# Thirteen down tiles of a PEER layer split in two parts instead of six

## The chip, the cores and the metric

The kernel runs on one core of a Trainium2 chip. The time is the device time of one execution in microseconds; before the change the median of three runs is 1321.99 us (1321.54 to 1322.99).

In what follows TensorE (PE) multiplies matrices, VectorE (DVE), ScalarE (ACT) and GpSimd (POOL) work elementwise, and SyncE (SP) issues most of the loads.

## The reference, cut to what matters

Two blocks run one behind the other on a sequence of 256 tokens with 1024 features, all in float32. The change lies in the last layer of the second block, a PEER layer: for each token eight heads pick 16 of 16384 one-neuron experts each.

```
qry = (ht @ w_query).reshape(T, 8, 2, 128)
sub_scores = einsum('thpc,hpkc->thpk', qry, sub_keys)
top_s, top_i = top_k(sub_scores, 16)
cand_s = top_s[:, :, 0, :, None] + top_s[:, :, 1, None, :]
best_s, best_c = top_k(cand_s.reshape(T, 8, 256), 16)
gate = softmax(best_s)
a = einsum('pd,ped->pe', xb, expert_down[ib])
act = gelu(a) * gb
y = einsum('pe,ped->pd', act, expert_up[ib])
```

## The kernel before

The kernel doesn't gather experts. It multiplies all 16384 rows of `expert_down` with all 256 tokens, in 128 tiles of 128 experts (a down tile), takes the Gelu, multiplies by a dense matrix G that holds each token's gates and is zero elsewhere, and multiplies with all rows of `expert_up`.

A float32 product comes in two forms. In the split form an operand is cut into an upper part `hi` (ScalarE, a copy to the type fp32r, line 218) and a lower part `lo` (GpSimd, source minus `hi`, line 220), and three matmuls per block of 128 features add hi by hi, hi by lo and lo by hi (`mm3`, lines 285 to 287). The layer's input stands in SBUF so already, as `xh` and `xl` (in the trace xTh and xTl). In the full-precision form one float32 matmul per block is issued (line 1561), straight from the loaded tile `dst`; its input is `xf`, the sum of `xh` and `xl`, made in four pieces by GpSimd (`xf_part`, line 1695).

The order around the change is the order in which the program is written; each engine runs its instructions in it.

- Query heads 0 to 7 (`q_mm`, `q_score`): TensorE makes scores, VectorE finds the best 16 (`top16`: MAX8, FIND_INDEX8, MATCH_REPLACE8), and GpSimd adds the candidate sums of an earlier head (`best_sums`, lines 1510 and 1513, four small instructions a head). The sums of the last head, 7, are VectorE's. Meanwhile GpSimd makes lower parts of query weights and of down tiles 0 and 1, and three of the four pieces of `xf`.
- Down tiles 0 to 11 (`down_step`, `NPRE` = 12). Step n first issues the split of tile n + 2, a half at a time, if n + 2 is below `SPLIT`, then the matmuls of tile n and its Gelu (line 1569). With `SPLIT` = 6, tiles 0 to 5 are split and tiles 6 to 25 full-precision. Upper and lower parts lie in four buffers each.
- Beside these steps, VectorE turns the chosen candidates into keys (`best_keys`): TENSOR_SCALARs of 128x128 (lines 1523 to 1528 and 1535) and predicated copies that walk down a binary tree (lines 1531 and 1540). Behind step 8 ScalarE takes the Exp of the gates (line 1487), and VectorE divides by their sum (lines 1489 to 1491).
- Behind tile 11, TensorE transposes keys and gates (`to_slots`, lines 1496 and 1497); ScalarE and VectorE (line 1504) copy them out.
- Tile 12, and then the one-hot rows: VectorE builds them in float16 (lines 1620 and 1627), TensorE multiplies them to G (line 1640), with down tiles 13 to 25 in between, a half tile at a time.
- From tile 26 on (`LEAD` = 26) a loop over all 128 tiles takes a split down tile and an up tile in each turn.

Of the kernel before, what the change touches and what calls it, by code (L numbers as in the profile page):

```python
# [32 lines left out]
    _off += _w  # L33
NCST = _off
LEAD = 26
SPLIT = 6


VEC = {}
# [45 lines left out]
def block_kernel(ctx: ExitStack, tc, a, dump=None, stop=None):  # L85
# [814 lines left out]
    def q_load(g):  # L900
        st = strm.tile([P, 8, 256], F32, tag="st", name=nm("st"))
        sp.dma_start(st, wq[:, g * 256:(g + 1) * 256].rearrange("(p j) n -> p j n", j=8))
        qprep[g] = st
# [12 lines left out]
    def q_split(g):  # L916
        q_hi(g)
        q_lo(g, 0, pool if g > 1 else vec)
        q_lo(g, 1)
# [331 lines left out]
    for s in range(28):  # L1251
        i, g = divmod(s, 2)
# [70 lines left out]
    for s in range(28, 36):  # L1323
        i, g = divmod(s, 2)
# [103 lines left out]
    def q_mm(g):  # L1428
        pr = qprep.pop(g)
        o = (MM if g else PSM)([P, 2, T])  # L1430
        for kk in (range(0, 4), range(4, 8)):
            for part, x in ((0, xh), (1, xh), (0, xl)):
                for k in kk:
                    for m in range(2):
                        pe.matmul(o[:, m, :], pr[k // 4][part][:, k % 4, m * P:(m + 1) * P], x[:, k, :],  # L1435
                                  start=k == 0 and m == 0 and part == 0 and x is xh,
                                  stop=k == KD - 1 and x is xl, skip_group_check=True)
        act.activation(qTs[g % 2], o, AF.Copy)
# [15 lines left out]
    def q_score(g):  # L1454
        sps = PSM([P, 2, 2, P])
        for tt in range(2):
            for i in range(2):
                pe.matmul(sps[:, tt, i, :], qTs[g % 2][:, i, tt * P:(tt + 1) * P], skT[:, g * 2 + i, :],
                          start=True, stop=True)
        sc = scr[g % 3]  # L1460
        act.activation(sc, sps, AF.Copy)
        top16([(tv[tt][:, g * 2 + i, :], ti[tt][:, g * 2 + i, :], sc[:, tt, i, :])
               for tt in range(2) for i in range(2)])
# [42 lines left out]
    def best_sums(h, eng):  # L1506

        for b in best:
            v0, v1 = tv[b.tt][:, 2 * h, :], tv[b.tt][:, 2 * h + 1, :]
            eng.tensor_tensor(b.cd[:, h, 0:64].rearrange("p (x y) -> p x y", x=4),  # L1510
                              v0[:, 0:4, None].to_broadcast([P, 4, 16]),
                              v1[:, None, :].to_broadcast([P, 4, 16]), op=ALU.add)
            eng.tensor_tensor(b.cd[:, h, 64:112].rearrange("p (x y) -> p x y", x=12),
                              v0[:, 4:16, None].to_broadcast([P, 12, 4]),
                              v1[:, None, 0:4].to_broadcast([P, 12, 4]), op=ALU.add)

    def best_top(h):
        top16([(b.bs[:, h, :], b.bc[:, h, :], b.cd[:, h, :]) for b in best])

    def best_keys(best):  # L1520

        for b in best:
            vec.tensor_scalar(b.g64, b.bc, 64, None, op0=ALU.is_ge)
            vec.tensor_scalar(b.rk[0], b.bc, 4, None, op0=ALU.logical_shift_right)
            vec.tensor_scalar(b.r2[0], b.bc, 2, None, op0=ALU.logical_shift_right)
            vec.tensor_scalar(b.rk[1], b.bc, 15, None, op0=ALU.bitwise_and)
            vec.tensor_scalar(b.r2[1], b.bc, 3, None, op0=ALU.bitwise_and)
            vec.tensor_scalar(b.r2[0], b.r2[0], 12, None, op0=ALU.subtract)
        for b in best:
            for side in range(2):  # L1530
                vec.copy_predicated(b.rk[side], b.g64, b.r2[side])
        for side in range(2):
            for b in best:
                for bi, w in enumerate((8, 4, 2, 1)):
                    vec.tensor_scalar(b.bit[bi], b.rk[side], w, None, op0=ALU.bitwise_and)
            for bi, w in enumerate((8, 4, 2, 1)):
                for b in best:
                    tree = b.tree[side]
                    data = b.tfh[:, :, side, None, 8:16].to_broadcast([P, 8, 16, 8]) if w == 8 else tree[:, :, :, w:2 * w]
                    vec.copy_predicated(tree[:, :, :, 0:w], b.bit[bi][:, :, :, None].to_broadcast([P, 8, 16, w]), data)  # L1540


    def down_load(i):
        st = strm.tile([P, 2, KD, P], F32, tag="st", name=nm("dst"))
        sp.dma_start(st.rearrange("p a k e -> p (a k e)"), down_w[i // 2])
        dload[i], dload[i + 1] = st[:, 0], st[:, 1]

    def down_split(i, half=None):
        if half != 1:
            dprep[i] = (dload.pop(i), *HL([P, KD, P]))  # L1550
        dT, hi, lo = dprep[i]
        s = slice(0, 8) if half is None else slice(half * 4, half * 4 + 4)
        split(hi[:, s, :], lo[:, s, :], dT[:, s, :], lo="pool")
# [139 lines left out]
    def xf_part(i):  # L1693
        s = slice(2 * i, 2 * i + 2)
        pool.tensor_tensor(xf[:, s], xh[:, s].bitcast(F32), xl[:, s].bitcast(F32), op=ALU.add)
# [4 lines left out]
    for g in range(8):  # L1700
        if g + 2 < 8:
            q_load(g + 2)
        else:
            down_load(2 * g - 12)
        if g + 1 < 8:
            q_split(g + 1)
        else:
            down_split(0)
        q_mm(g)
        if g > 1:  # L1710
            best_sums(g - 2, pool)
        if g == 7:
            xf_part(0)
            xf_part(1)
        if g:
            q_score(g - 1)
        if g > 1:
            best_top(g - 2)
    down_split(1)
    best_sums(6, pool)  # L1720
    xf_part(2)
    q_score(7)
    best_top(6)
    best_sums(7, vec)
# [3 lines left out]
    NPRE, N_COPY, N_GATE = 12, 3, 8  # L1728

    def down_step(n):  # L1730

        if n % 2 == 0 and n + 4 < LEAD:
            down_load(n + 4)
        yield
        if n + 2 < SPLIT:
            down_split(n + 2, 0)
        down_mm(n, 0)
        yield
        if n + 2 < SPLIT:
            down_split(n + 2, 1)  # L1740
        down_mm(n, 1)
        dload.pop(n, None)
        down_act(n)
        if n == LEAD - 3:
            down_load(LEAD)
        if n == LEAD - 2:
            up_load(0)
        yield

    for n in range(NPRE):  # L1750
        for part, _ in enumerate(down_step(n)):
            if part and 0 < n - N_COPY <= 2:
                best[part - 1].leaves(n - N_COPY - 1)
        if n == 1:
            xf_part(3)
        if n == N_COPY:
            for b in best:
                b.copies()
        if n == N_COPY + 2:
            best_keys(best)  # L1760
        if n == N_GATE:
            for b in best:
                b.gates()
# [84 lines left out]
    for tt in range(2):  # L1848
        for hf in range(2):
            n = 2 if tt and hf else 1  # L1850
# [30 lines left out]
```

## Time and profile before

| | us |
|---|---|
| median of three runs | 1321.99 |
| the profiled execution | 1321.84 |
| its span, first to last instruction | 1320.1 |
| TensorE busy in it | 1290.4 |
| VectorE busy | 828.7 |
| ScalarE busy | 675.8 |
| GpSimd busy | 381.7 |

Times in the trace count from the start of the span. The stages around the change are: query heads to about 537 us, down tiles 0 to 11 from 537 to 578, one-hot rows with tiles 12 to 25 from 578 to 657, then the loop over the 128 tiles. A row of the timeline has the start, the time taken, the engine, the line, the operation with output and inputs, and the count of instructions that were merged into it; in brackets stands the idle time ahead of it and the engine that ended it. A duration includes the time in which an instruction that has been started waits for a resource. Instructions on one engine overlap a little, so the pace is read from their starts.

### The profile page before, as it was taken

The numbers are of one execution on the slowest core, as the hardware profiler recorded it, in microseconds if no ns is written. First come the engines' busy times: TensorE is split into PE (matmuls) and PEld (weight loads), VectorE is DVE, ScalarE is ACT, GpSimd is POOL, SyncE is SP. The second block draws the span as 40 slices with busy tenths as digits, with TensorE's granted clock in tenths as the row PEclk, the third lists the DMA queues.
The fourth block names the chain that finished last, engine by engine and source line by source line (L and its number), as shares of the span: only waits on it lengthen the run. The fifth ranks groups of instructions, "written<-read, shape, count | busy, mean of one in ns | idle before, by whom it ended". The sixth has DMA issues, their size and how long they took to land.

```text
span 1320.1 us, 20727 instructions
## 1 busy us (share of the span) xinstructions
PE 1290.4 (98%) x8176; PEld 1141.3 (86%) x8176; DVE 828.7 (63%) x1522; ACT 675.8 (51%) x1146; POOL 381.7 (29%) x219
## 2 busy tenths in 40 slices
PE   7999999999999999999999999999999999999998
PEld 6877899977777879988889999999999999999886
DVE  6868788766866768989974754333333333333676
ACT  7755554544665454536654444544444444444442
POOL 0101111011212128700154444443444444444100
PEclk9999999999999999999999999999999999999999
DMA  9526679865564365346555665665555755455653
GB/s 302 200 81 238 222 257 299 304 245 192 170 208 162 125 187 166 129 141 201 193 210 214 229 228 194 244 255 192 192 191 187 276 210 179 178 185 191 214 184 112
DMA packets 103538, 266.73 MB, mean 202 GB/s; under 512 B 6873, under 2 KB 50571, under 8 KB 94993
## 3 DMA queue, kind: packets, MB, share of 16 engines
q1 hardware_dynamic: 93376, 255.32, 55.2%
q10 hardware_dynamic: 10064, 10.09, 2.3%
q8 instruction: 64, 1.05, 0.3%
q14 instruction: 34, 0.27, 0.1%
HBM read 254.90 MB, written 10.49 MB: 201 GB/s over the span
## 4 chain that ended last, share of the span: by engine, by line
PE 82%; DVE 9%; ACT 3%; issue 2%; DMA 2%; POOL 1%; ACTq 0%; SPq 0%; DVEq 0%; POOLq 0%
PE mm L287 12%; PE mm L286 12%; PE mm L285 12%; PE mm L299 9%; PE psm L285 7%; PE psm L287 7%; PE psm L286 7%; PE psm L1561 5%; PE mm L1640 2%; PE mm L758 2%; DVE lo L222 2%; DMA aw<-in_ada_w_dram 1%; PE mm L1435 1%; ACT hi L218 1%; DVE s L1448 1%
## 5 line engine op out<-in xcount | busy, mean ns | idle before, releaser
L220 POOL TENSOR_TENSOR lo<-dst,hi 128x1024 fp32r<-128x1024 f32 (+1 forms) x113 | 269.6, 2388 | 419.8 <-ACT hi L218 419.8
L1585 DVE TENSOR_TENSOR lo<-ust,hi 128x1024 fp32r<-128x1024 f32 x128 | 165.0, 1289 | 341.2 <-ACT hi L1580 341.2
L285 PE MATMUL psm<-xTh,hi 128*128 128x256 f32 x864 | 244.6, 283 | 0.0
L287 PE MATMUL psm<-xTh,lo 128*128 128x256 f32 x864 | 242.7, 281 | 1.7 <-POOL lo L220 1.5
L286 PE MATMUL psm<-xTl,hi 128*128 128x256 f32 x864 | 244.1, 282 | 0.0
L1580 ACT ACTIVATE hi<-ust 128x1024 fp32r<-128x1024 f32 x128 | 135.7, 1060 | 207.9 <-DMA ust<-in_peer_up_dram 108.5
L285 PE MATMUL mm<-hi,og 128*128 128x512 f32 x512 | 202.2, 395 | 1.2 <-ACT og L1596 1.2
L286 PE MATMUL mm<-lo,og 128*128 128x512 f32 x512 | 202.9, 396 | 0.0
L287 PE MATMUL mm<-hi,og 128*128 128x512 f32 x512 | 202.5, 396 | 0.3 <-DVE og L1601 0.3
L222 DVE TENSOR_TENSOR lo<-st,hi 128x1024 fp32r<-128x1024 f32 x127 | 157.8, 1264 | 61.6 <-ACT hi L218 61.4
L218 ACT ACTIVATE hi<-st 128x1024 fp32r<-128x1024 f32 x127 | 132.1, 1055 | 101.6 <-PE mm L299 47.0
L287 PEld LDWEIGHTS psm<-xTh,lo 128*128 128x128 f32 x864 | 164.2, 190 | 2.5 <-POOL lo L220 2.5
L285 PEld LDWEIGHTS psm<-xTh,hi 128*128 128x128 f32 x864 | 161.8, 187 | 4.8
L286 PEld LDWEIGHTS psm<-xTl,hi 128*128 128x128 f32 x864 | 162.2, 188 | 4.2
L1569 ACT ACTIVATE ga<-psm 128x256 f32<-128x256 f32 x128 | 49.0, 383 | 150.9 <-PE psm L287 123.8
L287 PEld LDWEIGHTS mm<-hi,og 128*128 128x128 f32 x512 | 96.2, 188 | 23.7 <-DVE og L1601 0.9
L218 ACT ACTIVATE hi<-dst 128x1024 fp32r<-128x1024 f32 (+1 forms) x113 | 114.1, 1014 | 0.9 <-ACT gst L1647 0.9
L285 PEld LDWEIGHTS mm<-hi,og 128*128 128x128 f32 x512 | 96.2, 188 | 20.0 <-ACT og L1596 1.4
L286 PEld LDWEIGHTS mm<-lo,og 128*128 128x128 f32 x512 | 96.2, 188 | 18.8
L1589 DVE TENSOR_TENSOR oj<-ga,G 128x256 f32<-128x256 f32 x128 | 92.4, 722 | 1.3 <-ACT G L1643 1.3
L1561 PE MATMUL psm<-xf,dst 128*128 128x256 f32 x320 | 75.0, 383 | 0.0
L1561 PEld LDWEIGHTS psm<-xf,dst 128*128 128x128 f32 x320 | 58.5, 190 | 6.8
(448 smaller groups left out, 2157.1 us busy)
## 6 DMA issues: line engine op xcount, KB each, us to landing
dst<-in_downT_dram SPq DMA_DIRECT2D x64, 1024.0 KB, 6.8
ust<-in_peer_up_dram SPq DMA_DIRECT2D x64, 1024.0 KB, 4.9
st<-in_w_in_dram SPq DMA_DIRECT2D x25, 1024.0 KB, 5.9
st<-in_w_gate_up_dram SPq DMA_DIRECT2D x22, 1024.0 KB, 7.7
aw<-in_ada_w_dram SPq DMA_DIRECT2D x40, 512.0 KB, 5.6
st<-in_w_down_dram SPq DMA_DIRECT2D x11, 1024.0 KB, 4.8
st<-in_w_out_dram SPq DMA_DIRECT2D x8, 1024.0 KB, 5.0
st<-in_peer_w_query_dram SPq DMA_DIRECT2D x8, 1024.0 KB, 5.8
```

The source lines that it names most:

```text
L218: act.activation(dst_hi, src, AF.Copy)
L220: pool.tensor_tensor(dst_lo, src, dst_hi.bitcast(F32), op=ALU.subtract)
L222: vec.tensor_sub(dst_lo, src, dst_hi.bitcast(F32))
L285: pe.matmul(out, lh, rh, start=start, stop=False, **kw)
L286: pe.matmul(out, lh, rl, start=False, stop=False, **kw)
L287: pe.matmul(out, ll, rh, start=False, stop=stop, **kw)
L299: pe.matmul(o[:, m, :], wk(k)[part][:, m * P:(m + 1) * P], x[:, k, :], start=k == 0 and m == 0 and part == 0 and x is xh, stop=k == KD - 1 ...
L1561: pe.matmul(gas[i], dload[i][:, k, :], xf[:, k, :], start=k == 0, stop=k == KD - 1)
L1569: act.activation(ga, gas[i], AF.Gelu)
L1580: act.activation(hi, st, AF.Copy)
L1585: vec.tensor_sub(lo, st, hi.bitcast(F32))
L1589: vec.tensor_tensor(wf, gas.pop(i), Gq[i // 32][:, :, i % 32], op=ALU.mult)
```

## The change

`SPLIT` goes from 6 to 13: tiles 6 to 12 are split like tiles 0 to 5. The four pieces of `xf`, which tile 13 is now the first to read, are made behind the lower parts of tile 12, in one place.

```diff
-SPLIT = 6
+SPLIT = 13
...
         q_mm(g)
         if g > 1:
             best_sums(g - 2, pool)
-        if g == 7:
-            xf_part(0)
-            xf_part(1)
         if g:
             q_score(g - 1)
...
     down_split(1)
     best_sums(6, pool)
-    xf_part(2)
     q_score(7)
...
-        if n == 1:
-            xf_part(3)
+        if n == NPRE - 2:
+            for i in range(4):
+                xf_part(i)
```

GpSimd's queue from the last pieces of query work on. Before, tiles 1 (a whole tile in one instruction) to 5 (`lo_5312` to `lo_5485`) stand among the pieces of `xf`, with the candidate sums of head 6; the next row is tile 26 (`lo_6849`):

```order
L1695 TENSOR_TENSOR xf<-xTh_4250,xTl_4251 128x512 x2
L220 TENSOR_TENSOR lo_5312<-dst_5101,hi_5311 128x1024
L1510 TENSOR_TENSOR G_4519<-G_4519 128x64
L1513 TENSOR_TENSOR G_4519<-G_4519 128x48
L1510 TENSOR_TENSOR G_4518<-G_4519 128x64
L1513 TENSOR_TENSOR G_4518<-G_4519 128x48
L1695 TENSOR_TENSOR xf<-xTh_4250,xTl_4251 128x512
L220 TENSOR_TENSOR lo_5383<-dst_5207,hi_5382 128x512 x2
L220 TENSOR_TENSOR lo_5416<-dst_5207,hi_5415 128x512 x2
L1695 TENSOR_TENSOR xf<-xTh_4250,xTl_4251 128x512
L220 TENSOR_TENSOR lo_5452<-dst_5380,hi_5451 128x512 x2
L220 TENSOR_TENSOR lo_5485<-dst_5380,hi_5484 128x512 x2
```

Now, behind the same candidate sums, GpSimd has tiles 2 (`lo_5380`) to 12 (`lo_5784`) in a row, and then all four pieces:

```order
L220 TENSOR_TENSOR lo_5380<-dst_5207,hi_5379 128x512 x2
L220 TENSOR_TENSOR lo_5413<-dst_5207,hi_5412 128x512 x2
L220 TENSOR_TENSOR lo_5448<-dst_5377,hi_5447 128x512 x2
L220 TENSOR_TENSOR lo_5481<-dst_5377,hi_5480 128x512 x2
L220 TENSOR_TENSOR lo_5518<-dst_5445,hi_5517 128x512 x2
L220 TENSOR_TENSOR lo_5553<-dst_5445,hi_5552 128x512 x2
L220 TENSOR_TENSOR lo_5638<-dst_5515,hi_5637 128x512 x2
L220 TENSOR_TENSOR lo_5671<-dst_5515,hi_5670 128x512 x2
L220 TENSOR_TENSOR lo_5706<-dst_5635,hi_5705 128x512 x2
L220 TENSOR_TENSOR lo_5749<-dst_5635,hi_5748 128x512 x2
L220 TENSOR_TENSOR lo_5784<-dst_5703,hi_5783 128x512 x2
L1695 TENSOR_TENSOR xf<-xTh_4250,xTl_4251 128x512 x4
```

Fourteen halves of lower parts (tiles 6 to 12) are new in GpSimd's queue, and the pieces of `xf` have moved behind them.

TensorE's order around the transposes, with the last two full-precision tiles ahead of them (10 and 11, outputs `psm_5687` and `psm_5698`) and tile 12 behind, before:

```order
L1561 MATMUL psm_5687<-xf,dst_5627 128x256 x8
L1561 MATMUL psm_5698<-xf,dst_5627 128x256 x8
L1496 MATMUL mm_5709<-cst,G_4519 128x128 x2
L1497 MATMUL mm_5709<-cst,G_4519 128x128
L1496 MATMUL mm_5716<-cst,G_4518 128x128 x2
L1497 MATMUL mm_5716<-cst,G_4518 128x128
L1561 MATMUL psm_5733<-xf,dst_5651 128x256 x8
```

and now, with the end of tile 11 (`psm_5820`) and the start of tile 12 (`psm_5871`):

```order
L285 MATMUL psm_5820<-xTh_4250,hi_5748 128x256
L286 MATMUL psm_5820<-xTl_4251,hi_5748 128x256
L287 MATMUL psm_5820<-xTh_4250,lo_5749 128x256
L1496 MATMUL mm_5847<-cst,G_4519 128x128 x2
L1497 MATMUL mm_5847<-cst,G_4519 128x128
L1496 MATMUL mm_5854<-cst,G_4518 128x128 x2
L1497 MATMUL mm_5854<-cst,G_4518 128x128
L285 MATMUL psm_5871<-xTh_4250,hi_5783 128x256
L286 MATMUL psm_5871<-xTl_4251,hi_5783 128x256
```

The transposes keep their place between tiles 11 and 12; only the form of the tiles around them is another. VectorE's order is the same as before.

## Rows read from the trace of the kernel before

**Rows 1.** One stretch: length, each engine's busy time and instructions, clock, DMA.

```profile
557.00:578.00 21.00, 21.00 (x101) 18.52 (x100) 18.22 (x61) 6.35 (x12) 0.00 (x0) 1.00 0.38 144
```

**Rows 2.** Timeline of ScalarE: an upper part, Gelus of tiles, the Exp's table load.

```profile
538.58 1.15 ACT L218 ACTIVATE hi<-dst 128x512 fp32r<-128x512 f32 x2
...
548.12 0.39 ACT L1569 ACTIVATE ga<-psm 128x256 f32<-128x256 f32 x1 [3.03 <-PE psm L287]
...
551.00 0.38 ACT L1569 ACTIVATE ga<-psm 128x256 f32<-128x256 f32 x1 [1.46 <-PE psm L287]
...
557.25 0.38 ACT L1569 ACTIVATE ga<-psm 128x256 f32<-128x256 f32 x1 [0.60 <-PE psm L287]
...
568.01 1.28 ACT L1487 ACT_TABLE_LOAD   x1
...
577.97 0.38 ACT L1569 ACTIVATE ga<-psm 128x256 f32<-128x256 f32 x1 [3.07 <-PE psm L1561]
```

**Rows 3.** Timeline of GpSimd in the same stage.

```profile
542.63 1.28 POOL L1695 TENSOR_TENSOR xf<-xTh,xTl 128x512 f32<-128x512 f32 x1
...
550.10 5.03 POOL L220 TENSOR_TENSOR lo<-dst,hi 128x512 fp32r<-128x512 f32 x4
```

**Rows 4.** TensorE, 540 to 600: waits (us in total, times, longest), then its timeline.

```profile
PE psm L287 <- POOL lo L220: 1.5, 2, 1.3
...
PE mm L1640 <- DVE og L1627: 1.4, 3, 0.7
...
578.32 0.27 PE L1497 MATMUL mm<-cst,G 128*128 128x128 f32 x1
...
585.63 1.94 PE L1561 MATMUL psm<-xf,dst 128*128 128x256 f32 x8
```

**Rows 5.** Timeline of VectorE from head 6's maxima to the gates.

```profile
551.12 0.43 DVE L1450 MAX8 G<-s 128x8 f32<-128x112 f32 x2
...
551.97 0.74 DVE L1510 TENSOR_TENSOR G<-G 128x64 f32<-128x64 f32 x1
552.64 1.31 DVE L1513 TENSOR_TENSOR G<-G 128x48 f32<-128x48 f32 x1
553.87 1.34 DVE L1510 TENSOR_TENSOR G<-G 128x64 f32<-128x64 f32 x1
555.14 0.20 DVE L1513 TENSOR_TENSOR G<-G 128x48 f32<-128x48 f32 x1
555.25 0.44 DVE L1444 MAX8 G<-G 128x8 f32<-128x112 f32 x2
...
557.43 0.48 DVE L1727 TENSOR_TENSOR G<-G 128x128 f32<-128x128 f32 x2
...
560.26 1.17 DVE L1535 TENSOR_SCALAR G<-G 128x128 uint32<-128x128 uint32 x8
561.34 5.93 DVE L1540 COPY_PREDICATED G<-G 128x1024 f32<-128x1024 uint32 x8
...
573.65 0.39 DVE L1489 TENSOR_REDUCE gsum<-G 128x8 f32<-128x128 f32 x1
...
575.09 0.29 DVE L1491 TENSOR_TENSOR G<-G,gsum 128x128 f32<-128x128 f32 x1
```

**Rows 6.** Line 1060 (ns min/median/max, starts), one of its instructions, and GpSimd beside it.

```profile
L1060 DVE TENSOR_SCALAR sss<-sss x4: 172/602/647, 341.5 to 361.6; 128x8 f32<-128x8 f32 x4
...
341.48 0.65 DVE L1060 TENSOR_SCALAR sss<-sss 128x8 f32<-128x8 f32 x1
...
340.80 1.29 POOL L1058 TENSOR_TENSOR sqs<-sqs,b_sb_q_gain 128x512 f32<-128x512 f32 x1 [6.43 <-ACT sqn L1057]
```

**Rows 7.** GpSimd, then VectorE, where tile 26 meets the one-hot rows.

```profile
654.27 6.04 POOL L220 TENSOR_TENSOR lo<-dst,hi 128x512 fp32r<-128x512 f32 x2 [99.14 <-ACT hi L218]
...
656.79 0.68 DVE L1627 TENSOR_TENSOR og<-oj,gate 128x1024 f16<-128x1024 f16 x1
```

**Rows 8.** Another stretch, columns as in the first group.

```profile
480.00:490.00 10.00, 9.32 (x65) 8.90 (x65) 7.36 (x10) 6.12 (x10) 1.88 (x1) 0.83 0.70 208
```

## The prediction

> **What bounds the kernel now.** I first read the stretch in which the tiles lie that change their form [rows 1]. From 557 to 578 us TensorE is busy all 21.00 us, so it gives something only if it must do less there; VectorE is nearly as full with 18.22 us, and GpSimd does nothing at all.
>
> Next, TensorE's pace, by the Gelu that ScalarE runs when a tile is complete [rows 2]. Two-part tiles follow each other at 551.00 - 548.12 = 2.88 us. The six full-precision tiles 6 to 11 take (577.97 - 557.25) / 6 = 3.45 us each. Before that TensorE lost 1.5 us waiting for the lower parts from GpSimd, 1.3 of it in one piece at tile 2, since the sums of the input parts stood ahead of that tile in GpSimd's queue [rows 3, 4].
>
> Last, who else must be ready when TensorE leaves tile 11. The transposes of the gates come behind tile 11 in TensorE's order; the last of them starts at 578.32 [rows 4]. They read VectorE's tree of keys and its gates, and VectorE's last instruction for these ends at 575.09 + 0.29 = 575.4 [rows 5]. So VectorE is 2.9 us ahead of the end of this stage: TensorE bounds it, with VectorE close behind. VectorE has no idle time from the small sums at 551.97 to there, so 575.4 comes earlier only if these instructions get shorter.
>
> **The change part by part.**
>
> *TensorE.* Tiles 6 to 11 save 6 x (3.45 - 2.88) = 3.4 us, and the 1.5 us of waits go if GpSimd keeps up, since the first two sums and the third no longer stand ahead of tiles 1 and 2. It frees TensorE 5 us earlier, at about 573. Tile 12 saves another 0.6 us, but behind it TensorE waits 1.4 us in all for VectorE's one-hot rows [rows 4], so that is counted at nothing; its cover is that wait.
>
> *ScalarE.* Fourteen more upper halves at 0.57 us (1.15 for two) [rows 2] are 8 us; ScalarE is busy 6.35 of 21 us there [rows 1], so this is hidden. They queue between the Gelus, and those of tile 11 stand behind the two Exp of the gates with a table load of 1.28 us ahead (568.01) [rows 2]. That only makes GpSimd pause a little over 1 us.
>
> *GpSimd.* Each half of a lower part takes 5.03 / 4 = 1.26 us and each sum of the input parts 1.28 [rows 3]. Without sums in between, it starts tile 2 at 542.6 and runs 2.5 us a tile against TensorE's 2.88, so TensorE need not wait for it. Tile by tile, with the upper parts that follow each Gelu: tiles 2 to 6 end at 555.1, tile 7 at 557.6, tile 8 starts at 558.1 when ScalarE has its upper half. After that it is all but full until the fourth sum ends near 577.5. Tile 13, the first to read the sums, started 7.3 us behind the last transpose (585.63) [rows 4], so the sums are in time.
>
> *VectorE.* No instruction is added or moved, but GpSimd now works beside the tree, where it was silent. What that costs is the term that decides. The four small sums at 551.97 run beside GpSimd already: they start 0.67, 1.23 and 1.27 us apart, each as one of GpSimd's halves ends, and the last, after GpSimd has finished, takes 0.20 [rows 3, 5]. A one-input TENSOR_SCALAR waits too: the shortest of line 1060 takes 172 ns, but the one started at 341.48, with GpSimd at work from 340.80 to 342.09, takes 650 and ends at 342.13 [rows 6]. The maxima and index searches do not wait: two MAX8 take 0.43 us beside GpSimd and 0.44 without it [rows 5]. So VectorE's instructions with two inputs, and the TENSOR_SCALARs, get in once per GpSimd instruction.
>
> The Trainium skill (SBUF — State Buffer, section "Who interferes with whom") has a rule that speaks against this change: a VectorE instruction with two inputs in SBUF, or a one-source one in a mode that uses both ports, and a GpSimd instruction shut each other out, each for a whole instruction. The rows agree for both kinds. By the rule the term is the +13.3 us worked out next; by the row where they part [rows 7] the +8.2 of the second rival.
>
> The predicated copies of the tree read a mask and data; no row shows one beside GpSimd.
>
> From 557.43 on nearly all of VectorE's work is of these kinds: 2 subtractions, 12 TENSOR_SCALARs, 4 copies, then twice 8 TENSOR_SCALARs and 8 larger copies [rows 5]. The sum:
> - The fourth small sum now meets a half of tile 7: + 1.25 - 0.13 = 1.1 us. The maxima behind it run beside GpSimd, and the exposed work starts at 558.6.
> - After that GpSimd still has the rest of one half (0.7), nine halves (tile 8's second to tile 12: 9 x 1.26 = 11.3) and four sums (4 x 1.28 = 5.1): 17.1 us, fourteen instructions, and VectorE gets one of its own in at each end. What it gets done so is its first short ones, at their pace of 0.135 us (1.17 for 8, with a tail) to 0.2: 14 x 0.15 = 2.1 us. Lost: 15.0 us.
> - VectorE ends at 575.4 + 1.1 + 15.0 = 591.5, the last transpose starts at 591.6 instead of 578.3: **+13.3 us**. TensorE, done at 573, waits some 19 us.
>
> Bounds of that term: below, - 2.9 us (nothing waits, TensorE's earlier end counts until VectorE's 575.4); above, 18.2 (no credit for what VectorE gets done). I take 13.3, since the four small sums are the nearest row and alternate exactly so. If the predicated copies do not wait, the first four pass and the second group of TENSOR_SCALARs takes the slots: VectorE ends near 590.4, +12.
>
> *Clock.* After such a wait TensorE may start again at its lower level. From 480 to 490 us, behind waits of TensorE, the mean granted clock was 0.83 [rows 8]; with levels of 1.2 and 2.4 GHz that is 3.4 us at the lower one, a loss of 1.7. It would fall on tile 12, which is 0.6 us shorter and has the 1.4 us of waits behind it: counted at nothing, 1.7 in the range.
>
> Sum: 1321.84 of the profiled execution (span 1320.1) + 13.3 = 1335.1; the median before is 0.15 above that run: **1335.3 us**.
>
> **The rivals.**
>
> *Nothing clashes* (the other side). The exposed instructions pass GpSimd freely. Then TensorE is done at 573, VectorE at 575.4 to 576.5, and the stage ends 1.8 to 2.9 us earlier: 1319.1 to 1320.2. It decides as long as VectorE loses under 2.9 us, fewer than three GpSimd instructions. Against it stand the waits above [rows 5, 6]. For it: no row shows a 128x128 TENSOR_SCALAR or a predicated copy beside GpSimd.
>
> *VectorE holds on.* When GpSimd came to the float16 one-hot stream at 654.27, it did not get in at each end: its two halves took 6.04 us instead of 2.5, the first finishing only after VectorE paused at 657.47 [rows 7]. If the tree does this, its exposed work (557.43 to 573.65, 16.2 us) runs through from 559.4, and GpSimd starts tile 8's second half only at 575.6. It then needs 1.25 x 7 = 8.8 us to the end of tile 11 (584.4), and TensorE follows with half a tile, 1.4: last transpose near 586.5, +8.2 us: 1330; more where the sums then meet the one-hot stream. Against it: at 552 VectorE's next sum was there at once too, and GpSimd got in.
>
> *Only one kind waits* (the one-input or the two-input ones): between 1331 and 1334.5, the copies' case above and its mirror.
>
> *TensorE's whole 5 us is gained*: 1316.6. Excluded by VectorE's 575.4. That the change does not split the tiles is excluded by the order of the instructions.
>
> **How the numbers follow.** Alternating: 0.56, at 1335.3. One kind only: 0.13. VectorE holds on: 0.16. Nothing clashes: 0.13. Rest: 0.02. The range takes in the first three with the clock and the missing credit above (1335.3 + 2.1 + 1.7 = 1339) and the held port with some of TensorE's savings below: 1328 to 1340. A difference under 0.2% (2.6 us) cannot be told from none. Nothing clashes falls on both sides of that bound, mostly inside: faster 0.04, same 0.11, slower 0.85.
>
> **What would show it.** Right: TensorE idle for 15 to 20 us ahead of the line-1496 transposes; GpSimd full from 558 to 577 with instructions of 1.25 us; line 1523 to 1528 spaced by about 1.25 us instead of 0.135; the tree's copies at their old length. Held port: GpSimd instructions of many us and TensorE waiting at line 287 for lower parts. Wrong: TENSOR_SCALARs still 0.135 us apart with GpSimd busy, and transposes at 576.

## The result and the profile after

The changed kernel takes 1334.68 us, the median of four runs (1333.0 to 1336.18), against 1322.0 for the kernel before beside it. The ratio is 1.0097, with a 95% interval of 1.0082 to 1.0111; of 1322.0 that is 12.8 us slower (10.8 to 14.7). Forecast were +13.3 us and 1335.3, with a range of 1328 to 1340.

The profiled execution of the changed kernel took 1333.0 us, its span 1331.2. Its stage of down tiles began a little earlier than in the trace of before. The mark for that is the first candidate sum of head 6 on GpSimd, in the trace of before:

```profile
541.68 0.29 POOL L1510 TENSOR_TENSOR G<-G 128x64 f32<-128x64 f32 x1 [1.00 <-DVE G L1450]
```

GpSimd's timeline after, from that mark on:

```profile
540.15 0.29 POOL L1510 TENSOR_TENSOR G<-G 128x64 f32<-128x64 f32 x1 [1.01 <-DVE G L1450]
...
541.10 22.87 POOL L220 TENSOR_TENSOR lo<-dst,hi 128x512 fp32r<-128x512 f32 x18
565.47 11.32 POOL L220 TENSOR_TENSOR lo<-dst,hi 128x512 fp32r<-128x512 f32 x4 [1.50 <-ACT hi L218]
576.75 4.92 POOL L1695 TENSOR_TENSOR xf<-xTh,xTl 128x512 f32<-128x512 f32 x4
```

The stage starts 541.68 - 540.15 = 1.53 us earlier, through nothing that the change touches: the candidate sums of the head before, ahead of every moved instruction, are 1.54 us earlier as well (533.30 against 534.84). All comparisons below therefore add 1.53 to times of after ("on before's clock"), and likewise for the experiments, each by its own mark.

Eighteen halves follow each other at 22.87 / 18 = 1.27 us, then GpSimd pauses 1.50 us for an upper part, and the next four halves take 11.32 us instead of 5.03 [rows 3]. With a narrower window of the same timeline, the first of these four alone:

```profile
565.47 6.99 POOL L220 TENSOR_TENSOR lo<-dst,hi 128x512 fp32r<-128x512 f32 x1 [1.50 <-ACT hi L218]
```

VectorE's timeline after, from the small sums of head 7 to the gates; it answers to [rows 5], where line 1727 is now 1723. Of before, two rows that are not among those come first:

```profile
559.45 0.91 DVE L1531 COPY_PREDICATED G<-G 128x128 uint32<-128x128 uint32 x4
...
566.89 1.30 DVE L1535 TENSOR_SCALAR G<-G 128x128 uint32<-128x128 uint32 x8
```

and after:

```profile
550.44 5.77 DVE L1510 TENSOR_TENSOR G<-G 128x64 f32<-128x64 f32 x1
...
556.38 1.30 DVE L1513 TENSOR_TENSOR G<-G 128x48 f32<-128x48 f32 x1
557.60 0.44 DVE L1444 MAX8 G<-G 128x8 f32<-128x112 f32 x2
...
559.79 1.78 DVE L1723 TENSOR_TENSOR G<-G 128x128 f32<-128x128 f32 x2
561.50 1.31 DVE L1523 TENSOR_SCALAR G<-G 128x128 uint32<-128x128 uint32 x1
562.73 1.32 DVE L1524 TENSOR_SCALAR G<-G 128x128 uint32<-128x128 uint32 x1
563.98 0.21 DVE L1525 TENSOR_SCALAR G<-G 128x128 uint32<-128x128 uint32 x1
...
566.13 1.17 DVE L1535 TENSOR_SCALAR G<-G 128x128 uint32<-128x128 uint32 x8
567.21 8.76 DVE L1540 COPY_PREDICATED G<-G 128x1024 f32<-128x1024 uint32 x8
575.59 6.57 DVE L1535 TENSOR_SCALAR G<-G 128x128 uint32<-128x128 uint32 x8
582.08 5.88 DVE L1540 COPY_PREDICATED G<-G 128x1024 f32<-128x1024 uint32 x8
...
589.01 0.29 DVE L1491 TENSOR_TENSOR G<-G,gsum 128x128 f32<-128x128 f32 x1
```

VectorE ends the gates at 589.01 + 0.29 = 589.30, on before's clock 590.83: 15.45 us later than 575.38 [rows 5]. TensorE's timeline from the end of tile 11, and one of its waits from 535 to 620 (us in total, times, longest); both answer to [rows 4]:

```profile
572.51 0.58 PE L287 MATMUL psm<-xTh,lo 128*128 128x256 f32 x1 [3.88 <-POOL lo L220]
...
573.10 0.41 PE L286 MATMUL psm<-xTl,hi 128*128 128x256 f32 x1
573.32 0.41 PE L287 MATMUL psm<-xTh,lo 128*128 128x256 f32 x1
...
576.37 0.28 PE L286 MATMUL psm<-xTl,hi 128*128 128x256 f32 x1
576.49 0.28 PE L287 MATMUL psm<-xTh,lo 128*128 128x256 f32 x1
576.61 0.28 PE L1496 MATMUL mm<-cst,G 128*128 128x128 f32 x1
587.46 0.48 PE L1496 MATMUL mm<-cst,G 128*128 128x128 f32 x1 [10.57 <-DVE G L1540]
...
589.36 0.47 PE L1497 MATMUL mm<-cst,G 128*128 128x128 f32 x1
589.49 0.56 PE L285 MATMUL psm<-xTh,hi 128*128 128x256 f32 x1
...
593.86 1.09 PE L1640 MATMUL mm<-og,oj 128*128 128x128 f16 x16
...
596.77 1.94 PE L1561 MATMUL psm<-xf,dst 128*128 128x256 f32 x8
```

```profile
PE mm L1640 <- DVE og L1627: 0.7, 2, 0.6
```

TensorE has done tile 11 at 576.6 and then waits 10.57 us for VectorE's tree. The last transpose starts at 589.36 against 578.32: on before's clock 12.57 us later. The first half of tile 13 starts at 596.77 against 585.63 [rows 4]: 12.67 later. Nothing behind it gives any of that back (the spans differ by 11.1 us, with the 1.53 that is 12.6), so the whole loss arises between the small sums of head 7 and the transposes. Three stretches (columns as in [rows 1]):

```profile
557.00:578.00 21.00, 16.00 (x120) 15.60 (x119) 21.00 (x53) 9.34 (x18) 19.50 (x12) 0.92 0.41 149
570.00:580.00 10.00, 4.38 (x23) 4.19 (x23) 10.00 (x10) 0.38 (x1) 10.00 (x7) 0.78 0.29 105
580.00:590.00 10.00, 1.88 (x7) 1.32 (x8) 9.44 (x20) 0.68 (x3) 1.67 (x2) 0.50 0.00 0
```

VectorE's 21.00 and GpSimd's 19.50 us are not work alone: an instruction that has started and is kept out counts as busy. In the last stretch, while TensorE waits, its granted clock is 0.50, its lower level.

### The profile page after: what moved, and what is told of

Its sections match the earlier page's. It is cut to its first block, busy times and chain, and to the rows that moved or that the text cites. A ratio compares the mean times of both kernels' runs of the same rounds, so it can differ in the third digit from the quotient of the medians.

```text
span 1331.2 us, 20871 instructions
## 1 busy us (share of the span) xinstructions
PE 1288.1 (97%) x8232; PEld 1142.1 (86%) x8232; DVE 842.8 (63%) x1522; ACT 683.1 (51%) x1160; POOL 408.3 (31%) x233
## 4 chain that ended last, share of the span: by engine, by line
PE 76%; DVE 14%; DMA 4%; ACT 3%; issue 2%; SPq 0%; POOL 0%; ACTq 0%; DVEq 0%; POOLq 0%
PE mm L287 12%; PE mm L286 12%; PE mm L285 12%; PE psm L285 7%; PE psm L286 7%; PE psm L287 7%; PE mm L299 7%; PE psm L1561 3%; PE mm L1640 2%; DVE lo L222 2%; PE mm L758 2%; DMA aw<-in_ada_w_dram 1%; DVE G L1540 1%; DMA st<-in_w_in_dram 1%; PE mm L1435 1%
## 5 line engine op out<-in xcount | busy, mean ns | idle before, releaser
L220 POOL TENSOR_TENSOR lo<-dst,hi 128x1024 fp32r<-128x1024 f32 (+1 forms) x127 | 296.0, 2338 | 406.2 <-ACT hi L218 322.1
L287 PE MATMUL psm<-xTh,lo 128*128 128x256 f32 x920 | 259.7, 282 | 4.1 <-POOL lo L220 3.9
L285 PE MATMUL psm<-xTh,hi 128*128 128x256 f32 x920 | 262.1, 285 | 0.0
L286 PE MATMUL psm<-xTl,hi 128*128 128x256 f32 x920 | 261.1, 284 | 0.0
L1580 ACT ACTIVATE hi<-ust 128x1024 fp32r<-128x1024 f32 x128 | 135.7, 1060 | 210.5 <-DMA ust<-in_peer_up_dram 110.4
L287 PEld LDWEIGHTS psm<-xTh,lo 128*128 128x128 f32 x920 | 176.3, 192 | 4.9 <-POOL lo L220 4.9
L285 PEld LDWEIGHTS psm<-xTh,hi 128*128 128x128 f32 x920 | 173.8, 189 | 4.8
L286 PEld LDWEIGHTS psm<-xTl,hi 128*128 128x128 f32 x920 | 174.1, 189 | 4.2
L218 ACT ACTIVATE hi<-dst 128x1024 fp32r<-128x1024 f32 (+1 forms) x127 | 122.5, 972 | 0.9 <-ACT gst L1647 0.9
L299 PE MATMUL mm<-xTh,hi 128*128 128x256 f32 x416 | 59.4, 284 | 0.3 <-ACT xTh L377 0.3
L299 PE MATMUL mm<-xTh,lo 128*128 128x256 f32 x416 | 58.8, 282 | 0.0
```

The costliest lines, as they stand in the source:

```text
L218: act.activation(dst_hi, src, AF.Copy)
L220: pool.tensor_tensor(dst_lo, src, dst_hi.bitcast(F32), op=ALU.subtract)
L285: pe.matmul(out, lh, rh, start=start, stop=False, **kw)
L286: pe.matmul(out, lh, rl, start=False, stop=False, **kw)
L287: pe.matmul(out, ll, rh, start=False, stop=stop, **kw)
L299: pe.matmul(o[:, m, :], wk(k)[part][:, m * P:(m + 1) * P], x[:, k, :], start=k == 0 and m == 0 and part == 0 and x is xh, stop=k == KD - 1 ...
```

## The experiments

Three theories run through them. A: whatever GpSimd does beside VectorE's exposed instructions (two inputs, or TENSOR_SCALAR) is paid by VectorE, and VectorE's end sets the transposes. B: VectorE passes freely. C: something else sets the loss, such as TensorE's wait for lower parts. All of them are read off the same two events, on before's clock; the timed difference is the ratio applied to the time of the kernel before beside it:

| kernel | mark | gates end | last transpose | its shift | timed difference (95%) |
|---|---|---|---|---|---|
| before | 541.68 | 575.38 | 578.32 | | |
| after | 540.15 | 590.83 | 590.89 | +12.6 | +12.8 (10.8 to 14.7) |
| e1_sums_before | 543.05 | 588.16 | 588.22 | +9.9 | +8.2 (5.5 to 10.7) |
| e5_sums_first | 541.40 | 586.52 | 586.58 | +8.3 | +8.9 (5.9 to 11.9) |
| e2_work14 | 542.72 | 588.95 | 589.01 | +10.7 | +12.6 (7.8 to 17.3) |
| e3_work6 | 543.93 | 580.43 | 580.49 | +2.2 | +1.2 (-0.7 to 3.0) |
| e4_memset14 | 541.98 | 584.00 | 584.06 | +5.7 | +5.2 (3.3 to 6.9) |
| e6_split8 | 540.19 | 583.14 | 583.20 | +4.9 | +5.0 (3.3 to 6.9) |
| e7_no_lower | 543.17 | 575.55 | 575.61 | -2.7 | -1.9 (-3.3 to -0.4) |

The shift of the last transpose accounts for the timed difference within 2 us in every row.

**GpSimd's work alone, in two doses.** The kernel before, unchanged but for additions of 128x512 on GpSimd that nobody reads, put beside the tree. Fourteen:

```diff
+    dmy = pb.tile([P, 2, T], F32, name="dmy", bufs=1)
+    def idle_work():
+        pool.tensor_tensor(dmy, xh[:, 0:2].bitcast(F32), xl[:, 0:2].bitcast(F32), op=ALU.add)
...
             if part and 0 < n - N_COPY <= 2:
                 best[part - 1].leaves(n - N_COPY - 1)
+            if part < 2 and 4 <= n <= 10:
+                idle_work()
```

> The kernel before (six tiles split), with fourteen additions of half a tile (128x512) on GpSimd beside the tree, at the places of the new lower parts; they write a scratch tile that nobody reads. Theory A: nothing but GpSimd being busy makes the loss. The additions run from 555.1 to 573; VectorE is kept from its two-input and TENSOR_SCALAR instructions for 17.9 - 2.3 (beside the maxima) + 1.1 (fourth small sum) - 1.9 (what it gets done) = 14.8 us, of which 2.9 are its lead on TensorE: + 11.9, 1333.9 us, range 1330 to 1336. Theories B and C (the moved sums, or lower parts that come late): 1322, since neither is there.

And six (`4 <= n <= 6`):

> A smaller dose of the run with 14 additions: the kernel before with six additions of 128x512 on GpSimd, read by nobody, put behind the lower parts of tiles 6 to 8. Six at 1.28 us fill GpSimd to about 563, some 4.4 us beyond the point where VectorE's exposed work starts. Theory A (every GpSimd instruction beside the tree is paid by VectorE, the path is shared and its work adds up): VectorE loses about 4.6 us, of which 2.9 are its lead: +1.7, 1323.2 us where the kernel before is at 1321.4 (1322 to 1325.5), and TensorE waits about 1.7 us for VectorE at the line-1496 transposes. Theory B (VectorE is not slowed by GpSimd): no difference, and no such wait. Theory C (the loss is a fixed price of meeting at all, not in proportion to the work): as much as with 14 additions, 1334.

Measured: 1334.37 us (ratio 1.0095, 1.0059 to 1.0131) and 1322.74 us (1.0009, 0.9995 to 1.0023), both inside A's ranges; by its time alone the smaller dose can't be told from none. Fourteen idle additions, with TensorE's part of the change left out, cost as much as the whole change within the intervals; by the last transpose they cost 10.7 of the 12.6 us. GpSimd's and VectorE's timelines with fourteen:

```profile
556.11 19.25 POOL L1700 TENSOR_TENSOR dmy<-xTh,xTl 128x512 f32<-128x512 f32 x14
```

```profile
561.77 1.29 DVE L1523 TENSOR_SCALAR G<-G 128x128 uint32<-128x128 uint32 x1
562.97 0.21 DVE L1524 TENSOR_SCALAR G<-G 128x128 uint32<-128x128 uint32 x1
563.11 1.29 DVE L1525 TENSOR_SCALAR G<-G 128x128 uint32<-128x128 uint32 x1
...
569.84 3.05 DVE L1531 COPY_PREDICATED G<-G 128x128 uint32<-128x128 uint32 x4
```

The TENSOR_SCALARs get in two at a time, one pair per addition, and the four small predicated copies, 0.91 us in the kernel before, take 3.05: the operation that no row of before showed beside GpSimd waits too. The two doses give a price: eight additions more move VectorE's end from 580.43 to 588.95, 8.52 us, or 1.07 for each 1.28 us of GpSimd. Theory C of the smaller dose (a fixed price of meeting at all) is out; B is out by the larger dose. With six, VectorE loses 5.05 us, but 2.9 of that is its lead, so only 2.2 show in the trace, where TensorE now waits 1.5 us for VectorE at lines 1496 and 1497.

**The same, but GpSimd reads nothing.** Fourteen memsets of 128x1280, 17.31 / 14 = 1.24 us each, in the same places (`pool.memset(dmy, 0.0)`).

> As the run with fourteen additions, but with fourteen memsets of 128x1280 (about 1.2 us each), which read nothing. Theory A1 (what is shared is the way by which GpSimd reads, for two-input instructions, and both ways for TENSOR_SCALARs): the predicated copies pass, the TENSOR_SCALARs wait one memset each, and VectorE loses about 12 us before its lead: 1331, range 1328 to 1333. Theory A2 (only reads clash): no instruction waits, 1322. Theory A3 (any GpSimd instruction shuts VectorE out): as with the additions, 1332 to 1334.

Measured: 1326.44 us (1.0039, 1.0025 to 1.0052). GpSimd's and VectorE's timelines:

```profile
555.39 17.31 POOL L1700 MEMSET dmy<- 128x1280 f32 x14
```

```profile
557.75 0.46 DVE L1732 TENSOR_TENSOR G<-G 128x128 f32<-128x128 f32 x2
...
559.06 1.26 DVE L1525 TENSOR_SCALAR G<-G 128x128 uint32<-128x128 uint32 x1
559.19 1.20 DVE L1526 TENSOR_SCALAR G<-G 128x128 uint32<-128x128 uint32 x1
...
565.30 0.89 DVE L1531 COPY_PREDICATED G<-G 128x128 uint32<-128x128 uint32 x4
566.11 4.27 DVE L1535 TENSOR_SCALAR G<-G 128x128 uint32<-128x128 uint32 x8
570.30 5.93 DVE L1540 COPY_PREDICATED G<-G 128x1024 f32<-128x1024 uint32 x8
```

The two kinds part here. Subtractions and predicated copies, which read two inputs, pass the memsets at their free length (0.46, 0.89, 5.93, of which the memsets, done at 572.70, cover the first 2.4 us); the one-input TENSOR_SCALARs are kept out as before, two per memset. The pattern expected of A1 held; the time came out under its range (1328 to 1333), because two got in each time and not one.

**Only the sums moved.** The change (`SPLIT` = 13) with the pieces of `xf` back where they were before (e1), and with all four ahead of the query heads (e5), so that only the halves meet the tree. The diff is that of e5 against the changed kernel; e1 has the old places instead of the first two lines:

```diff
+    for i in range(4):
+        xf_part(i)
     best = [Best(0, c2_), Best(1, c1_)]
...
-        if n == NPRE - 2:
-            for i in range(4):
-                xf_part(i)
```

> Thirteen tiles split as in the changed kernel, but the four sums of the input parts stay at their places of before. Theory A (GpSimd's work beside VectorE's tree of keys adds to the tree's time, whichever of the two is served first): the tree's stretch loses four sums (5.1 us) and gains two halves of lower parts that the sums push into it (2.6), so the stage ends 2.6 us earlier than in the changed kernel: 1332.1 us, range 1330 to 1334. Theory B (the sums in their new place are what costs): back to the time of before or 3 us below it, 1319 to 1323. Theory C (TensorE's wait for a late lower part, 3.9 us in the changed kernel's trace, is what costs): unchanged or later, 1334 to 1337, since the lower parts come later still.

> Thirteen tiles split, and all four sums of the input parts ahead of the query heads, where GpSimd has had no work for 14 us. Theory A: the tree's stretch loses the four sums and nothing else changes in it: 5.1 us less than the changed kernel, 1329.6 us, range 1327 to 1332; up to 5 us more if the sums hold up the query heads. Theory B: 1322 or less. Theory C: 1334 or a little less.

Measured: 1329.84 us (1.0062, 1.0042 to 1.0081) and 1330.18 us (1.0067, 1.0045 to 1.009). The first is 0.2 us under A's range, the second inside it; by the last transpose they gain 2.7 and 4.3 us on the changed kernel, where A had 2.6 and 5.1. TensorE's longest wait for a lower part is 3.9 us in both, as in the changed kernel, so neither B nor C holds. The place of the sums accounts for 2.7 to 4.6 us of the loss, by the transposes and by the times, and the fourteen halves for the rest. VectorE's small sums in e1, and the first of them in e5:

```profile
553.35 0.74 DVE L1510 TENSOR_TENSOR G<-G 128x64 f32<-128x64 f32 x1
554.01 1.31 DVE L1513 TENSOR_TENSOR G<-G 128x48 f32<-128x48 f32 x1
555.24 1.34 DVE L1510 TENSOR_TENSOR G<-G 128x64 f32<-128x64 f32 x1
556.51 1.31 DVE L1513 TENSOR_TENSOR G<-G 128x48 f32<-128x48 f32 x1
```

```profile
551.65 5.84 DVE L1510 TENSOR_TENSOR G<-G 128x64 f32<-128x64 f32 x1
```

In e1 the small sums alternate with GpSimd's halves one by one, as in [rows 5]; in e5, against the same halves, the first sum is kept out for 5.84 us. The first larger copies of the tree then keep GpSimd out in both (8.78 and 8.76 us for eight). The way in which the two share differs; the end does not by much.

**Half of the change.** `SPLIT` = 8, with the four sums behind tile 7.

> Half of the change: tiles up to 7 in two parts (not 12), the four sums of the input parts behind the lower part of tile 7. TensorE saves two tiles' 0.57 us and the waits of 1.5, 2.6 in all, and is done at 575.7. GpSimd is busy to about 563. Theory A (VectorE pays for GpSimd's work beside its tree): VectorE ends near 580, +1.7: 1323.2 us where the kernel before is at 1321.4 (1322 to 1325.5). Theory B (TensorE's time decides, VectorE passes GpSimd): VectorE's 575.4 and TensorE's 575.7 give 1318.8 (1318 to 1320). Theory C (TensorE's wait for lower parts decides): the wait at line 287 is 3 us or more and TensorE does not wait for VectorE at line 1496.

Measured: 1325.37 us (1.0038, 1.0025 to 1.0052): inside A's range, but at its upper end. VectorE's end moved by 7.8 us where A had 4.6. GpSimd's timeline behind the halves, and VectorE's first small sum, show why:

```profile
556.14 5.04 POOL L1695 TENSOR_TENSOR xf<-xTh,xTl 128x512 f32<-128x512 f32 x4
```

```profile
550.45 10.82 DVE L1510 TENSOR_TENSOR G<-G 128x64 f32<-128x64 f32 x1
```

The first small sum is kept out until GpSimd has nothing left (its fourth sum ends at 556.14 + 5.04 = 561.18). Behind it in VectorE's order stand the maxima, which could have run beside GpSimd, and they lose the time as well.

**TensorE's side alone.** Tiles 6 to 12 in two parts, but their lower parts are not made: the products read the lower part of tile 5.

```diff
+        if 6 <= i < 13:
+            if half != 1:
+                dprep[i] = (dload.pop(i), strm.tile([P, KD, P], F32R, tag="hi", name=nm("hi"), bufs=4), dprep5[0])
...
+            act.activation(hi[:, s, :], dT[:, s, :], AF.Copy)
+            return
```

> TensorE's side of the change alone. Tiles 6 to 12 are multiplied in two parts as in the change, and ScalarE makes their upper parts, but GpSimd makes no lower parts for them: their products read the lower part of tile 5 (this leaves out part of what is computed). The sums stay where they were before, so GpSimd is silent beside the tree. Theory A (all of the loss is GpSimd's work beside VectorE's tree): TensorE is done with tile 11 at 578.3 - 3.4 = 574.9, VectorE ends its gates at 575.4 as before and bounds the stage: -2.8, 1318.6 us where the kernel before is at 1321.4 (1317.6 to 1319.6), with a short wait of TensorE for VectorE. Theory B (ScalarE's fourteen upper halves, queued between Gelus, Exps and the table load, hold TensorE up): 1320 to 1325, with waits of TensorE at line 285 or 287 for ScalarE. Theory C (two parts do not save time on TensorE): 1321.4 or more.

Measured: 1319.84 us beside 1321.74 of before (0.9986, 0.9975 to 0.9997), 0.2 us above A's range, with A's gain of 2.8 inside the interval (0.4 to 3.3). TensorE's timeline, first the row of before that it answers to:

```profile
577.77 0.38 PE L1496 MATMUL mm<-cst,G 128*128 128x128 f32 x2
```

```profile
575.81 0.40 PE L1496 MATMUL mm<-cst,G 128*128 128x128 f32 x2
...
577.10 0.33 PE L1497 MATMUL mm<-cst,G 128*128 128x128 f32 x1 [0.21 <-DVE G L1491]
```

The transposes can start at 575.81 - 1.49 = 574.3 on before's clock, 3.4 us earlier than before, and the last one then waits for VectorE, which ends as before (575.55). What TensorE saves is real, and all that it can bring is VectorE's lead. ScalarE's added upper halves, rival B of this run, held nobody up: TensorE has no wait for ScalarE in this stage.

**Versions for gain.** If GpSimd has to be silent beside the tree, what fits ahead of it? Tried were the four sums ahead of the query heads with `SPLIT` 6 and 7 (v1, v4), and `SPLIT` 7 with the third sum ahead of head 6's candidate sums and the fourth behind tile 6 (v2).

> A version for gain: the kernel before (tiles up to 5 in two parts) with all four sums of the input parts ahead of the query heads, where GpSimd has time. Theory A (only what GpSimd does beside VectorE's two-input and TENSOR_SCALAR instructions costs): the lower parts of tiles 2 to 5 come 1.3 to 5 us earlier, TensorE's 1.5 us of waits for them go, and GpSimd is silent before VectorE's exposed work starts: -1.5, 1320.2 us where the kernel before is at 1321.7 (1319 to 1321.5). Rival (four sums ahead of the heads hold up the lower parts of the heads' weights): TensorE waits at line 287 there, 1322 to 1326.

> The same with tile 6 in two parts too (SPLIT 7). GpSimd's ten halves then end near 553.7 of the kernel before's time, where its fourth half with the sums between ended at 555.1, so VectorE ends at 575.4 to 575.9. Theory A: TensorE saves 1.5 us of waits and 0.57 of the tile, done at 576.2: -2.1, 1319.6 us where the kernel before is at 1321.7 (1318.5 to 1321). Rival (VectorE's first small sum is kept out until all ten halves are done, and its tree starts later by more than its 2.9 us of lead): 1322 to 1325, with TensorE waiting for VectorE at line 1496.

> A version for gain: one more tile (6) in two parts, the third sum of input parts ahead of head 6's candidate sums and the fourth behind tile 6's lower part, so that GpSimd ends its extra work near 557.7, before VectorE's exposed work starts at about 558.6. Theory A (only GpSimd's work beside the tree costs): TensorE saves 0.57 us and most of the 1.5 us of waits for lower parts, VectorE loses at most 1.1: about -1.5 to -2, 1319.6 us where the kernel before is at 1321.4 (1318.5 to 1321.5). Theory B (the earlier sum holds up the candidate sums, and VectorE's maxima with them): +0.5 to +1.5, 1322 to 1323.

v1 took 1320.02 us (ratio 0.9996, 0.9983 to 1.0008), v4 1319.5 (0.9991, 0.9975 to 1.0007), both beside 1320.07 of before: the gain expected was 1.5 to 2.1 us and can't be told from none. v2 took 1319.52 beside 1321.74 (0.9986, 0.9976 to 0.9996): 1.9 us faster, the only version whose interval is clear of none, and by less than 0.2%. In its trace the last transpose is 1.1 us earlier (575.85, with the first Gelu, its mark, at 539.68 against 541.05). In those of v1 and v4 it is 1.7 and 2.3 us earlier (573.55 with the mark at 538.62, 575.97 with 541.61), as forecast, so the traces don't put v2 first; which of the three is fastest stays open.

## Why the prediction was right, step by step

**What bounds the kernel: right.** VectorE's lead of 2.9 us is what every run turned on. e7 gained about that and no more, e3 lost its 5.05 us less that lead.

**VectorE, the term that decides: the sum was right, the way to it was not.** Forecast was 16.1 us (1.1 + 15.0), measured 15.45. But the step "VectorE gets one of its own in at each end" of a GpSimd instruction failed in the first half of the stretch. By the rows of after against [rows 5]:

| piece | forecast | measured |
|---|---|---|
| four small sums | +1.1 | +3.9 |
| two subtractions and twelve TENSOR_SCALARs | +15.0 | +1.3 and +2.2 |
| first eight larger copies | 0 | +2.8 (8.76 for 5.93) |
| second eight TENSOR_SCALARs | 0 | +5.3 (6.57 for 1.30) |
| second eight larger copies | 0 | 0 (5.88) |

The first small sum was kept out for 5.77 us, over more than four of GpSimd's halves. Then, when GpSimd paused 1.50 us for ScalarE (565.47), VectorE ran through: ten TENSOR_SCALARs at 0.135 us, and behind them copies, and GpSimd's next half took 6.99 us. Later they alternated at one GpSimd instruction per VectorE instruction.

The forecast total came out near because the sum priced GpSimd's queue and not the order: in e1 and e5, with other orders, the same reckoning gave 2.6 and 5.1 us less, and 2.7 and 4.3 were measured. That is argued from totals, and some luck is in it. Here the maxima behind the small sums still ran beside GpSimd, as forecast (from 557.60 on); in e6 they did not, and VectorE lost 3.2 us more than the sum gave, their 2.2 us (561.56 to 563.74) among them. The two doses confirm the rate: 1.07 us per GpSimd instruction measured, 15.0 / 14 = 1.07 forecast.

The rule that the prediction took from the Trainium skill (SBUF — State Buffer, "Who interferes with whom"), shut out for a whole instruction, agrees with the total and with the alternation from 575.59 on, but not with a sum kept out over more than four instructions; there the measurement decides. That the section excepts, for two-input instructions, a GpSimd instruction that only writes agrees with e4: two subtractions took 0.46 us beside memsets and 1.78 beside halves.

By the prediction's own signs, the mechanism was only half right. The first TENSOR_SCALARs were spaced by about 1.25 us (561.50, 562.73, 563.98). But TensorE did not idle for 15 to 20 us, and the tree's first eight larger copies did not keep their old length (8.76), while both signs of the held port were there: a GpSimd instruction of many us (6.99) and TensorE waiting at line 287 (3.88). The upper bound of 18.2 us is VectorE's loss with its lead not taken off, unlike the lower bound; the range goes by the 2.1 us of credit and is not touched by it.

**The predicated copies: open in the prediction, now shown.** They wait (3.05 us for four beside additions, 0.89 beside memsets). The prediction's case in which they pass did not occur.

**TensorE: wrong, but hidden.** "It frees TensorE 5 us earlier, at about 573": it was done at 576.61, on before's clock 578.1, no earlier than before. The step that failed is "GpSimd ... pause a little over 1 us" with "TensorE need not wait for it": the pause was 1.50 us as said, but it let VectorE in, the half behind it took 6.99, and TensorE waited 3.88 us for that lower part. Twelve matmuls followed at 0.213 us instead of 0.120, 1.1 us more, with a granted clock of 0.78 from 570 to 580. The sum 573.0 + 3.9 + 1.1 = 578.0 agrees with the 578.1 measured. GpSimd lost 6.99 - 1.26 = 5.7 us itself: its fourth sum ended at 576.75 + 4.92 = 581.67, on before's clock 583.2, and not near 577.5, still in time for tile 13. This is the mechanism of the rival "VectorE holds on", at a part of its size; it ended before VectorE did and cost nothing. From the end of tile 11 to the last transpose 589.36 - 576.61 = 12.75 us passed, 10.57 of them in one wait, and not some 19.

**Clock: right.** Tile 12 ran partly at the lower level (granted clock 0.50 from 589.5 to 592.5): 593.86 - 589.49 = 4.4 us to the first one-hot rows, 1.5 us more than a split tile's 2.88, where the prediction had 1.7. The waits for one-hot rows behind it fell from 1.4 us [rows 4] to 0.7, and tile 13 starts 12.67 us late where the last transpose was 12.57: it cost 0.1.

**The rivals.** "Nothing clashes" is refuted by e2, and its time, 1319.1 to 1320.2, is what e7 measured without GpSimd's part (1319.84). "Only one kind waits" is refuted for additions and halves; for memsets e4 shows it.

## What to carry to other kernels

Before work is given to an idle GpSimd, look at what VectorE does beside it. If these are TENSOR_SCALARs, or instructions with two inputs while GpSimd's read too, and VectorE is within a few us of the end of the stage, add most of GpSimd's time to VectorE's (here 1.07 us for each addition of 1.28), and subtract VectorE's lead. The sum came out near in most orders of the two, but not in all: whatever stands in VectorE's order behind an instruction that is kept out is kept out with it, even if it could have run. In e6 VectorE lost 3.2 us more than the sum, 2.2 of them by its maxima.

## What the runs showed of the hardware beyond that

GpSimd and VectorE don't simply alternate: against streams of 1.26 us halves, VectorE's small sums got in one per half in e1 (1.31, 1.34, 1.31 us), and the first of them was kept out for 5.77, 5.84 and 10.82 us in the changed kernel, e5 and e6. What decides between the two, no run here tells. It is not the work ahead alone: in e2 GpSimd and VectorE have the same instructions as before up to there, and the sum starts as far into a half (0.62 us, before 0.63); yet before it was through in 0.74 us [rows 5], and in e2 it was kept out:

```profile
553.00 4.52 DVE L1510 TENSOR_TENSOR G<-G 128x64 f32<-128x64 f32 x1
```

TENSOR_SCALARs got in one per half (1.31 and 1.32 us in the changed kernel, 1.32 in e1), but in pairs beside additions (1.29 and 0.21) and beside memsets (1.26 and 1.20). Predicated copies wait beside a GpSimd instruction that reads (3.05 us for four) and pass beside one that only writes (0.89).
